# A two-layer hybrid decoder step on one Trainium2 core: the product of Y and its gate Z in the SSD stage moves from GpSimd to VectorE

## The chip, the core and the metric

The kernel runs on one core of one Trainium2 chip. The metric is the device time of one execution in microseconds (us); lower is better. "TensorE clock" below is the granted clock of a stretch as a share of full speed: it has two levels, 1.2 and 2.4 GHz, so 1.00 means 2.4 GHz throughout and 0.50 means 1.2 GHz throughout.

## What is computed

One inference step of a trunk of two layers: a chunked gMLP mixer, an MLP, a Mamba-2 (SSD) mixer, an MLP, each with RMSNorm and adaLN shift, scale and gate. 256 prompt rows and 64 sample rows (8 sequences of 8) go through the same weights, so the kernel holds 320 columns (T = 320) at a time. The change is in the Mamba-2 mixer:

```
zxbcdt = h @ w_in
z, xbc, dt_raw = split(zxbcdt)
xs, bm, cm = split(silu(conv(xbc)))
y, new_ssm = ssd_scan(xs, dt, a, bm, cm, ssm_state)
y = y + xs * d_skip
y = y * silu(z)
yg = rms_norm(y per group of 256 channels, norm_g)
out = yg @ w_out
```

The line `y = y * silu(z)` is the one whose engine changes.

## The kernel before

All activations stand transposed, channels on the 128 partitions and the 320 rows on the free axis. Weights stream from HBM in tiles of 128 x 1024 fp32 (`raw`, a ring of 6). Each is split into a high part `whi` (ScalarE, L134) and a low part `wlo` (VectorE, L135) and multiplied in three passes, `mm3` (L299, L300, L301), into one of three PSUM banks `mm`. So every weight tile costs one ScalarE and one VectorE instruction before TensorE may use it, and a `raw` buffer comes free, and the next load may start on the queue of SyncE, when its `wlo` is made.

The SSD stage (from L561) has 8 groups of 4 heads. `convs(g)` (L763) makes the six projected tiles of a group: B, C and two X tiles through the causal convolution `conv` (L594; VectorE L608, GpSimd copies L598 to L603), and two gate tiles Z by Silu (L774). `ssd(g)` (L636) is a generator in six pieces, and the next group's `convs` steps it between its tiles, so that the scan of group g is written between the projections of group g+1. Its pieces: the C-B product (L640) and the decay matrix `bc` (loaded by L632, ScalarE L646 and L647, VectorE L648); transposes (L656, L658, L670 to L676) and their scalings (L683 to L688); chunk states (L694 to L699) and `cp` (L704); then the output Y:

- L716: TensorE adds up Y of each half in PSUM, with the recurrent `state` of the samples (`st`) as one factor.
- L727: VectorE adds `xs * d_skip`, 128 x 320, twice, into the tile Y (128 x 640).
- **L728: GpSimd multiplies Y by Z in place, 128 x 640, once per group.**
- L733: ScalarE squares Y (into Z), L735: VectorE adds the halves, and the RMS norm follows: TensorE sums (L202), VectorE makes the reciprocal root (L222 and L187 to L191, ten instructions on 128 x 3), TensorE spreads it (L197), VectorE writes the normed halves into `yst` (L739).
- L744 and L760: VectorE decays and updates the state `st` with the products of L753, and GpSimd's queue sends it out (L761).

From L850 on the finished groups are split into `hhi`/`hlo` and `yhi`/`ylo` (`ysplit`, ScalarE L830, VectorE L831) and multiplied by the output weights; the last two groups' scans run beside that. This switch is called the hand-over below.

The order of the instructions on each engine is set when the program is built: a scheduler with a time model of its own places them, engine by engine, within what the dependences allow. Moving one instruction to another engine can therefore change the order of many others. At run time each engine works through its list in order.

Of the kernel before, what the change touches and what calls it, by code (L numbers as in the profile page):

```python
# [12 lines left out]
ADD, SUB, MUL, MIN, MAX = ALU.add, ALU.subtract, ALU.mult, ALU.min, ALU.max  # L13
# [37 lines left out]
def tile_trunk(ctx: ExitStack, tc: tile.TileContext, io):  # L51
    nc = tc.nc
    pe, act, dve, pool = nc.tensor, nc.scalar, nc.vector, nc.gpsimd
# [570 lines left out]
    def yt(shape, tag, dtype=F32):  # L624
        return yp.tile(shape, dtype, tag=tag, name=nm(tag), bufs=2)
# [10 lines left out]
    def ssd(g_, st, bc, ea, B, C, X, Z):  # L636
# [71 lines left out]
        Y = yt([P, 2, T], "Y")  # L708
        for r in range(2):
# [15 lines left out]
                    mmy(slice(TP + LS * b, TP + LS * b + LS), lambda w: st[:, b, w], lambda h: cp[:, h, P + LS * b : P + LS * b + LS], False)  # L725
            dd = vec[:, V_D + 2 * g_ + r : V_D + 2 * g_ + r + 1]
            dve.scalar_tensor_tensor(Y[:, r], X[r], dd, py[:, :T], MUL, ADD)  # L727
        pool.tensor_tensor(Y, Y, Z, MUL)  # L728

        yield  # L730

# [86 lines left out]
    for hf in range(2):  # L818
        pe.transpose(pt[:, hf * P : (hf + 1) * P], stkd[:, hf, :], ident)
    act.copy(natS, pt.rearrange("p (h c) -> p h c", c=P)[:, 0:2, 64:96])  # L820
    prev = ssd(0, *group_loads(0), *cz)
    for g_ in range(1, NG):
        ld = group_loads(g_)
        cz = convs(g_, prev)
        for _ in prev:
            pass
        prev = ssd(g_, *ld, *cz)
# [238 lines left out]
```

## Time and profile before

| | |
|---|---|
| median of 3 runs | 1106.19 us (1102.05 to 1108.08) |
| the profiled execution, its own time | 1104.12 us |
| its span, first to last instruction | 1102.3 us |
| TensorE busy / weight loads | 1055.1 us (96%) / 971.5 us (88%) |
| VectorE, ScalarE, GpSimd busy | 658.6, 547.1, 315.9 us |
| mean granted TensorE clock | 0.982 |
| L728 on GpSimd | 8 instructions, 3.53 to 6.42 us each |

Times in the profile count from the span's start. A timeline row reads: start, duration, engine, line, operation, output<-inputs, shape of output<-shape of input, count; a bracket at its end gives how long the engine sat idle before it and what ended that. Durations of neighbours on one engine overlap a little, since a row also holds the write-back of its result. A row of waits reads: engine and line that waited, line it waited for, total us, times, longest.

### The profile page before, as it was taken

To read this page: it belongs to the slowest core of one execution; us is meant where nothing else is said; L and a number is where in the kernel's file an instruction comes from. 1 tells how busy PE (TensorE), PEld (TensorE's weight loads), DVE (VectorE), ACT (ScalarE), POOL (GpSimd) and SP (SyncE) were. 2 spreads that over 40 slices of the span, in tenths; PEclk is the share of its full clock that TensorE was granted. 3 is DMA by queue.
4 is the path that set the end of the run, shared out by engine and by line. 5 is a ranking of instruction groups with operands and counts; after the bars stand their busy time and mean duration, and the time that the engine had idled before them with its cause. 6 is when DMAs were issued, how large, how long until landed. Compare 5 with 4: busy or idle time off the path is not lost.

```text
span 1102.3 us, 19778 instructions
## 1 busy us (share of the span) xinstructions
PE 1055.1 (96%) x7809; PEld 971.5 (88%) x7809; DVE 658.6 (60%) x1080; ACT 547.1 (50%) x1013; POOL 315.9 (29%) x403
## 2 busy tenths in 40 slices
PE   5999999999999999999997989999899999999996
PEld 3677899889899889999996879999899899999996
DVE  3544956445744433445995898988866764443342
ACT  4443333434544433334879666787435455543331
POOL 1200124332333312113361343434325243320111
PEclk9999999999999999999998998999999999999998
DMA  8877885675777767545444555655445565444531
GB/s 330 305 234 231 282 316 186 213 245 177 239 216 219 220 219 222 169 145 194 131 149 152 204 199 191 207 200 203 144 140 183 180 216 167 153 147 143 152 95 48
DMA packets 60877, 213.97 MB, mean 194 GB/s; under 512 B 6560, under 2 KB 12128, under 8 KB 58480
## 3 DMA queue, kind: packets, MB, share of 16 engines
q1 hardware_dynamic: 58544, 200.47, 55.5%
q0 software_dynamic: 1952, 11.98, 3.1%
q8 instruction: 61, 1.00, 0.4%
q14 instruction: 32, 0.26, 0.1%
q10 hardware_dynamic: 288, 0.26, 0.1%
HBM read 199.31 MB, written 12.85 MB: 192 GB/s over the span
## 4 chain that ended last, share of the span: by engine, by line
PE 71%; ACT 8%; DVE 6%; issue 5%; DMA 4%; POOL 3%; POOLq 0%; ACTq 0%; SPq 0%; DVEq 0%
PE mm L299 19%; PE mm L301 18%; PE mm L300 18%; PE adap L157 4%; ACT bc L646 2%; ACT whi L134 2%; DVE wlo L135 2%; DVE co L608 1%; DMA bc<-rowd 1%; PE ax L716 1%; PE mm L403 1%; PE mm L404 1%; PE mm L405 1%; POOL Y L728 1%; PE ax L299 1%
## 5 line engine op out<-in xcount | busy, mean ns | idle before, releaser
L135 DVE TENSOR_TENSOR wlo<-raw,whi 128x1024 fp32r<-128x1024 f32 (+1 forms) x243 | 297.2, 1224 | 225.1 <-ACT whi L134 224.1
L134 ACT ACTIVATE whi<-raw 128x1024 fp32r<-128x1024 f32 (+1 forms) x243 | 254.8, 1050 | 277.2 <-PE mm L300 197.9
L299 PE MATMUL mm<-hhi,whi 128*128 128x320 f32 x952 | 305.4, 321 | 11.1 <-ACT cb L601 5.3
L300 PE MATMUL mm<-hlo,whi 128*128 128x320 f32 x952 | 298.8, 314 | 0.9 <-DVE hlo L831 0.8
L301 PE MATMUL mm<-hhi,wlo 128*128 128x320 f32 x952 | 298.4, 314 | 0.0
L299 PEld LDWEIGHTS mm<-hhi,whi 128*128 128x128 f32 x952 | 182.0, 191 | 29.0 <-issue 13.0
L300 PEld LDWEIGHTS mm<-hlo,whi 128*128 128x128 f32 x952 | 182.5, 192 | 2.0 <-DVE hlo L831 1.1
L301 PEld LDWEIGHTS mm<-hhi,wlo 128*128 128x128 f32 x952 | 182.0, 191 | 0.7 <-issue 0.2
L299 PE MATMUL mm<-mhi,whi 128*128 128x320 f32 x512 | 159.1, 311 | 0.0
L301 PE MATMUL mm<-mhi,wlo 128*128 128x320 f32 x512 | 158.1, 309 | 0.0
L300 PE MATMUL mm<-mlo,whi 128*128 128x320 f32 x512 | 157.9, 308 | 0.0
L350 POOL TENSOR_TENSOR ta<-ta 128x320 f32<-128x320 f32 x64 | 81.5, 1275 | 142.3 <-ACT ta L348 126.8
L299 PEld LDWEIGHTS mm<-mhi,whi 128*128 128x128 f32 x512 | 96.1, 188 | 4.1 <-issue 4.1
L300 PEld LDWEIGHTS mm<-mlo,whi 128*128 128x128 f32 x512 | 96.1, 188 | 0.0
L301 PEld LDWEIGHTS mm<-mhi,wlo 128*128 128x128 f32 x512 | 96.1, 188 | 0.0
L285 POOL TENSOR_TENSOR x<-x,rs 128x64 f32<-128x64 f32 x28 | 12.1, 431 | 222.8 <-DVE rs L284 222.8
L351 ACT ACTIVATE mhi<-ta 128x320 fp32r<-128x320 f32 x64 | 30.1, 470 | 79.1 <-POOL ta L350 79.1
L352 DVE TENSOR_TENSOR mlo<-ta,mhi 128x320 fp32r<-128x320 f32 x64 | 34.7, 548 | 53.7 <-ACT mhi L351 53.7
L608 DVE SCALAR_TENSOR_TENSOR co<-cb,vec,co 128x344 f32<-128x344 f32 x96 | 54.5, 580 | 7.4 <-ACT co L606 7.2
L157 PE MATMUL adap<-raw,sc 128*32 128x256 f32 x640 | 52.9, 390 | 0.2 <-DMA raw<-ada_w 0.2
L602 POOL COPY cvp<-cb 128x3 f32<-128x3 f32 x32 | 24.1, 753 | 70.3 <-ACT cb L600 70.2
L282 DVE SCALAR_TENSOR_TENSOR x<-mm,mod,x 128x256 f32<-128x256 f32 x29 | 14.0, 483 | 46.5 <-PE mm L301 45.2
(340 smaller groups left out, 1752.0 us busy)
## 6 DMA issues: line engine op xcount, KB each, us to landing
raw<-mlp_w SPq DMA_DIRECT2D x128, 512.0 KB, 3.9
raw<-ada_w SPq DMA_DIRECT2D x80, 512.0 KB, 4.4
raw<-w_in SPq DMA_DIRECT2D x48, 512.0 KB, 3.6
raw<-ada SPq DMA_DIRECT2D x16, 512.0 KB, 5.9
raw<-gm_wv SPq DMA_DIRECT2D x16, 512.0 KB, 5.5
raw<-gm_wu SPq DMA_DIRECT2D x16, 512.0 KB, 5.5
raw<-gm_wo SPq DMA_DIRECT2D x16, 512.0 KB, 4.5
st<-state SPq DMA_DIRECT2D x8, 1024.0 KB, 5.5
```

The costliest lines, as they stand in the source:

```text
L134: act.activation(hi[:, :n], raw[:, :n], AF.Copy)
L135: eng.tensor_tensor(lo[:, :n], raw[:, :n], hi[:, :n].bitcast(F32), SUB)
L157: pe.matmul(ps[32 * j : 32 * j + 32, :256], lhsT=sc[:, k, :], rhs=r[:, j * 256 : (j + 1) * 256], start=(k == 0), stop=(k == KD - 1), skip_ ...
L299: pe.matmul(ps[:, :n], lhsT=whi[:, kk, :], rhs=hi, start=first, stop=False)
L300: pe.matmul(ps[:, :n], lhsT=whi[:, kk, :], rhs=lo, start=False, stop=False)
L301: pe.matmul(ps[:, :n], lhsT=wlo[:, kk, :], rhs=hi, start=False, stop=last)
L350: pool.tensor_tensor(s, t, t, MUL)
L351: act.activation(mhi[:, m, :], s, AF.Copy)
L352: dve.tensor_tensor(mlo[:, m, :], s, mhi[:, m, :].bitcast(F32), SUB)
L602: pool.tensor_copy(cvp[:, ct, :], cb[:, TP : TP + 3])
L608: dve.scalar_tensor_tensor(o[:, :CO], cb[:, k : k + CO], wv(k), o[:, :CO], MUL, ADD)
L646: act.activation(bc[:, h, cq[c]], bc[:, h, cq[c]], AF.Relu, bias=nat[:, c, HG * g_ + h : HG * g_ + h + 1], scale=-1.0)
```

## The change

One line: the product is issued on VectorE's queue instead of GpSimd's. Shapes, operands and result are the same.

```diff
             dve.scalar_tensor_tensor(Y[:, r], X[r], dd, py[:, :T], MUL, ADD)
-        pool.tensor_tensor(Y, Y, Z, MUL)
+        dve.tensor_tensor(Y, Y, Z, MUL)
```

The scheduler orders other instructions anew from the first group's Y on. Three places matter below; + is a row of the changed program, - one of the program before, the others stand in both.

VectorE at the end of group 0 and the start of group 1. `cp` is the scaled C, `st` the state, `ta` the sum of squares (L735), `cbm` the masked C-B product.

```order
 L704 TENSOR_TENSOR cp_6174<-ea_5497,Ct_5609 128x768
 L608 SCALAR_TENSOR_TENSOR co_6448<-cb_6441,vec,co_6448 128x344
+L728 TENSOR_TENSOR Y_5787<-Y_5787,Z_5378 128x640
 L760 TENSOR_TENSOR st_5488<-st_5488,ax_5899 128x2x256
 L760 TENSOR_TENSOR st_5488<-st_5488,ax_5901 128x2x256
 L760 TENSOR_TENSOR st_5488<-st_5488,adap_5902 128x2x256
 L760 TENSOR_TENSOR st_5488<-st_5488,ax_5900 128x2x256
-L735 TENSOR_TENSOR ta_5874<-Z_5378 128x320
 L608 SCALAR_TENSOR_TENSOR co_6448<-cb_6441,vec,co_6448 128x344
 L642 TENSOR_TENSOR cbm_5972<-ax_5968,cst 128x320
```

The product stands behind `cp` and ahead of the state's updates, and the sum of squares moves back, to three rows beyond this piece.

ScalarE at the hand-over. `hhi` and `yhi` are high parts of the finished groups, `Z<-Y` is the square (L733) of group 6, `Z_8286` a gate tile of group 7.

```order
-L830 ACTIVATE hhi<-yst_5248 128x320 x5
-L733 ACTIVATE Z_7864<-Y_8319 128x640
-L830 ACTIVATE hhi<-yst_5248 128x320 x2
+L830 ACTIVATE hhi<-yst_5248 128x320 x7
 L134 ACTIVATE whi_8589<-raw_8587 128x1024
 L774 ACTIVATE Z_8286<-mm_8373 128x320
 L830 ACTIVATE hhi<-yst_5248 128x320
+L733 ACTIVATE Z_7864<-Y_8319 128x640
 L830 ACTIVATE yhi<-yst_5249 128x320 x4
```

The square moves back by five instructions: it now stands behind all eight `hhi`, a weight split and the gate tile.

ScalarE in group 2, where the gate of group 3 (`Z_6598`) is made from the banks `mm_6599` and `mm_6685`; `cb_6797` is a convolution input, `Bn`, `Bst` and `dup` are copies for group 2's scan.

```order
-L774 ACTIVATE Z_6598<-mm_6599 128x320
-L774 ACTIVATE Z_6598<-mm_6685 128x320
+L134 ACTIVATE whi_6966<-raw_6964 128x1024
+L600 COPY cb_6797<-mm_6766 128x256
+L601 COPY cb_6797<-mm_6766 128x8x8
 L660 COPY Bn_6467<-adap_6462 128x256
 L662 ACTIVATE Bst_6469<-adap_6462,cst 128x256
 L574 COPY dup_6878<-Bt_6387 128x256
 L574 COPY dup_6880<-Xt_6515 128x256
+L774 ACT_TABLE_LOAD
+L774 ACTIVATE Z_6598<-mm_6599 128x320
```

The gate tile, which frees a PSUM bank for TensorE, moves back behind seven instructions.

## Rows read from the trace of the kernel before

**Rows 1.** The page: busy time, share of the span and instructions of each engine.

```profile
PE 1055.1 (96%) x7809; PEld 971.5 (88%) x7809; DVE 658.6 (60%) x1080; ACT 547.1 (50%) x1013; POOL 315.9 (29%) x403
```

**Rows 2.** Busy us by stretch: PE, PEld, DVE, ACT, POOL, clock, DMA share, GB/s.

```profile
607.00:776.00 169.00, 160.23 (x1482) 150.53 (x1481) 149.89 (x269) 121.35 (x271) 65.90 (x94) 0.96 0.58 201
776.00:814.00 38.00, 34.29 (x293) 31.70 (x292) 27.77 (x54) 13.38 (x28) 8.99 (x5) 0.96 0.38 128
814.00:1078.00 264.00, 263.85 (x1826) 259.05 (x1825) 140.98 (x199) 122.58 (x194) 76.00 (x81) 1.00 0.50 158
656.00:668.00 12.00, 11.62 (x46) 10.22 (x46) 10.01 (x14) 8.72 (x21) 4.69 (x5) 0.57 0.46 173
784.00:792.00 8.00, 5.12 (x28) 5.03 (x27) 5.38 (x10) 4.63 (x10) 0.74 (x2) 0.79 0.26 98
```

**Rows 3.** What TensorE waited for from 607 to 814 us.

```profile
PE mm L299 <- ACT Z L774: 4.7, 2, 2.9
PE ax L640 <- DVE st L760: 2.0, 2, 1.6
PE nrm L197 <- DVE nv L191: 1.4, 2, 1.1
PE adap L672 <- DVE Bst L663: 1.4, 1, 1.4
PE nrm L202 <- DVE ta L735: 1.3, 2, 0.9
PE mm L300 <- DVE hlo L831: 0.8, 1, 0.8
```

**Rows 4.** Timeline of GpSimd: the product in groups 0, 4 and 6.

```profile
608.00 3.54 POOL L728 TENSOR_TENSOR Y<-Y,Z 128x640 f32<-128x640 f32 x1 [2.91 <-DVE Y L727]
...
714.45 4.42 POOL L728 TENSOR_TENSOR Y<-Y,Z 128x640 f32<-128x640 f32 x1 [1.85 <-DVE Y L727]
...
777.74 6.42 POOL L728 TENSOR_TENSOR Y<-Y,Z 128x640 f32<-128x640 f32 x1 [3.85 <-DVE Y L727]
```

**Rows 5.** Timeline of VectorE beside it: state decay and cp, groups 0 and 4.

```profile
607.83 2.29 DVE L744 TENSOR_TENSOR st<-st,ea 128x2048 f32<-128x2048 f32 x1
610.03 2.32 DVE L704 TENSOR_TENSOR cp<-ea,Ct 128x768 f32<-128x768 f32 x1
...
714.29 2.28 DVE L744 TENSOR_TENSOR st<-st,ea 128x2048 f32<-128x2048 f32 x1
...
716.49 0.95 DVE L704 TENSOR_TENSOR cp<-ea,Ct 128x768 f32<-128x768 f32 x1
```

**Rows 6.** VectorE: another product of two SBUF tiles, smaller.

```profile
615.15 0.48 DVE L735 TENSOR_TENSOR ta<-Z 128x320 f32<-128x320 f32 x1
```

**Rows 7.** Timeline of ScalarE in group 5 and at the hand-over.

```profile
751.08 0.74 ACT L733 ACTIVATE Z<-Y 128x640 f32<-128x640 f32 x1 [4.41 <-POOL Y L728]
...
776.55 2.06 ACT L830 ACTIVATE hhi<-yst 128x320 fp32r<-128x320 f32 x5
784.19 0.74 ACT L733 ACTIVATE Z<-Y 128x640 f32<-128x640 f32 x1 [5.58 <-POOL Y L728]
784.84 0.81 ACT L830 ACTIVATE hhi<-yst 128x320 fp32r<-128x320 f32 x2
785.55 1.04 ACT L134 ACTIVATE whi<-raw 128x1024 fp32r<-128x1024 f32 x1
786.50 0.41 ACT L774 ACTIVATE Z<-mm 128x320 f32<-128x320 f32 x1
```

**Rows 8.** Timeline of VectorE and of TensorE at the hand-over.

```profile
780.64 2.09 DVE L831 TENSOR_TENSOR hlo<-yst,hhi 128x320 fp32r<-128x320 f32 x5
...
781.18 0.41 PE L300 MATMUL mm<-hlo,whi 128*128 128x320 f32 x1 [0.83 <-DVE hlo L831]
...
786.97 0.64 PE L299 MATMUL mm<-hhi,whi 128*128 128x320 f32 x1 [2.88 <-ACT Z L774]
```

**Rows 9.** What the DMA queue of SyncE waited for from 607 to 814 us.

```profile
SPq L145 <- DVE wlo L135: 85.5, 16, 12.6
...
SPq L629 <- DMA o_ss<-st: 16.1, 6, 4.0
```

## The prediction, made before the changed kernel ran

> **What bounds the kernel now.** I read the busy times first: TensorE is busy 96% of the span, so only what makes TensorE wait, or run at its lower clock, can be won or lost [rows 1]. Then the stretches. From the first Y at 607 us to the hand-over at 776 us TensorE is busy 160.2 of 169 us, and VectorE is close behind with 149.9; from 776 to 814 us TensorE is busy 34.3 of 38; from 814 to 1078 us 263.85 of 264 [rows 2]. So the change can act between 607 and 814 us alone: there lie 12.5 us without TensorE work (8.8 + 3.7). The clock adds something: 0.96 in both stretches, and its worst piece, 656 to 668 us, has 0.57, which costs 12 x 0.43 = 5.2 us against full clock; the piece from 784 to 792 us has 0.79, that is 8 x 0.21 = 1.7 us [rows 2]. Then what TensorE waits for: most of it is VectorE's work, and the longest single wait, 2.9 us, is for a gate tile from ScalarE [rows 3]. Last I followed the product itself with its two neighbours.
>
> **Why the product is long on GpSimd.** It takes 3.54 us in group 0, 4.42 in group 4 and 6.42 in group 6 for the same 640 elements [rows 4]. In group 0 it starts at 608.00 while VectorE runs the state's decay, which ends at 610.12; the product ends at 611.54, 1.42 us after that. VectorE's next instruction, `cp`, starts at 610.03 and takes 2.32 us, while the same instruction takes 0.95 us in group 4 [rows 5]. So one waits for the other: the product for the decay, then `cp` for the product. In group 4 `cp` goes first and the product pays. In group 6 it starves behind a chain of VectorE products until 782.73 and ends at 784.16 [rows 4, 8]. The Trainium skill ("SBUF — State Buffer", section "Who interferes with whom") says that a VectorE instruction with two SBUF inputs and a GpSimd instruction that reads SBUF exclude each other for the whole instruction. These rows agree, to within the 0.95 against 2.32 us.
>
> **The change, step by step.**
>
> *Removed: 8 GpSimd products.* GpSimd is not what anything else waits for, except through the two effects below. Its queue keeps the copies of `conv` and the DMA of the state (L761), which now starts no later than VectorE's last update plus one or two copies: cost nothing, since the load of the next state that waits for it (6 waits, 16.1 us [rows 9]) also moves behind one more weight load in the new order, and its use moves later with the scan. If that cover fails, one wait of up to 4.0 us per group is exposed.
>
> *Added: 8 VectorE products of 128 x 640.* The trace has no such row. From below: 128 x 320 takes 0.48 us [rows 6]; from above: 128 x 768 takes 0.95 us [rows 5]. Between them, by elements, 0.48 + 320 x 0.47/448 = 0.82 us. I take 0.82, nearer the larger. Eight make 6.6 us.
>
> *Returned: the block on `cp`.* 2.32 - 0.95 = 1.37 us in each of groups 0 to 3 (four such rows of 2.31 or 2.32; group 0's and a free one are shown [rows 5]), 5.5 us in all. In groups 0 to 3 VectorE thus gains 1.37 - 0.82 = 0.55 us each. The updates of the state come that much earlier, and TensorE's two waits for them (1.6 and 0.4 us [rows 3]) shrink by 0.55 and 0.4: **-1.0 us**.
>
> *Groups 4 and 5.* Nothing is returned there; VectorE's list grows by 0.82 us each. What waits behind it on that engine are `wlo` tiles, and the loads behind those (85.5 us of waiting in 16 [rows 9]). At least 0, at most 1.6 us; since VectorE has about a tenth of the time idle and the new order moves `wlo` tiles forward, I take the middle, **+0.8 us**.
>
> *The hand-over, group 6.* Before, the square of group 6 stands in ScalarE's list ahead of two `hhi`, a weight split and a gate tile, and ScalarE sits 5.58 us until GpSimd is done. The gate tile ends at 786.9 and TensorE, which needs its bank, stands 2.88 us [rows 7, 8]; then it runs at 0.79 for a while (1.7 us). In the new order the square stands behind these. Seven `hhi` at 0.41, a split of 1.04 and a gate of 0.41 from 776.55 end at about 780.9, before TensorE needs the bank. What is late next is `hlo`: VectorE's product stands ahead of the seven, so TensorE's wait of 0.83 us grows by 0.82. Sum: -2.88 - 1.7 + 0.82 = **-3.8 us**. The two waits, 0.83 and 2.88, are all of the 3.7 us that TensorE is idle from 776 to 814 us, and later it has none to speak of [rows 2], so this stays won.
>
> *The norm chain.* The square no longer waits for GpSimd (4.41 us of ScalarE in group 5 [rows 7]), and the new order puts the sums (L202) and the spread (L197) later among the weight products. Their waits on VectorE are 1.3 and 1.4 us [rows 3]. I count the first as gone and half of the second, **-2.0 us** (bounds 0 and -2.7), since in group 1 the spread now stands inside the small products of L716 and may wait there.
>
> *Gate tiles of groups 2 to 4.* They move back on ScalarE behind work worth some 3 us. The wait for them is 4.7 - 2.88 = 1.8 us, once, now [rows 3]. I leave it as it is; bounds 0 and 2 x 1.8.
>
> *The clock.* The fall at 656 us follows the small products of L716 and a wait of 1.1 us for the norm chain. In the new order that place has no such wait, but group 1 has a like one. One fall stays: 0, with bounds -5.2 and +5.2.
>
> **Sum:** -1.0 + 0.8 - 3.8 - 2.0 = -6.0 us. Against the profiled execution's own 1104.1 that is 1098.1. The median of the runs shown stands 2.1 us above that execution, so I give 1100.2 for the median.
>
> **Rivals.**
>
> *Given back inside the stage (no change that can be told).* The hand-over is won, but the scheduler's new order, which rests on a time model and not on this chip, costs elsewhere: the gate tiles wait twice as long (+1.8), the norm chain keeps its waits (+2.0 against my sum), one more fall of the clock (+5.2 at most). For it: in the stretch to 776 us three engines are close to each other [rows 2], so an order that helps one hurts another. Against it: the waits that TensorE has now are mostly on VectorE, which does not get more work there. Time: with +3.8 it is 1104.0; with the half of a clock fall, 1106.6.
>
> *VectorE sets the pace (slower).* Place: groups 0 to 5, the queue of `wlo` tiles. VectorE is busy 149.9 of 169 us. If `cp` is not released, because GpSimd's copies for the convolutions take the place of the product, all of 6 x 0.82 = 4.9 us comes on top; every microsecond delays a `wlo` and the load behind it, and TensorE's stops bring one or two more falls of the clock (+5.2 each). With the hand-over won, 4.9 + 10.4 - 3.8 = +11.5: 1117.7. It decides from the point where TensorE's waits on `wlo` (none in [rows 3]) appear. The Trainium skill ("Perfetto Trace Analysis", section "Optimizing Scalar/DVE Operations") speaks against the change in the same sense: where VectorE is saturated, some work may better go to another engine, GpSimd included; the same paragraph doubts the pair VectorE and GpSimd because they share a port. By the first half the eight products alone would cost 6.6 us; by the second, nothing. The rows on `cp` side with the second half in four groups of eight.
>
> *The clock is won too (faster).* The fall at 656 us goes and no other comes: -6.0 - 5.2 = -11.2, 1095.0.
>
> That the product stays on GpSimd is ruled out by the order of the changed program.
>
> **How the numbers follow.** A measurement of this kernel can tell about 0.5% from no change, 5.5 us. Faster by more means below 1100.7. The sum as it stands and the case with the clock: 0.34 and 0.14, together 0.48. Given back: 0.38. VectorE sets the pace: 0.14. The range runs from 1093 (the clock case with the remaining waits for VectorE gone, -2) to 1108.5 (given back, with most of a clock fall); it leaves out most of the slower case and little at the bottom. My forecast lies close to the border, which is why the two first chances are near each other.
>
> **What would show it.** After: eight VectorE rows of 128 x 640 at about 0.82 us; all `cp` near 0.95; no ScalarE wait on GpSimd's Y; at the hand-over one TensorE wait of about 1.6 us for `hlo` in place of 0.8 and 2.9; VectorE's busy time up by about 1 us over the stage; TensorE idle between the first Y and 814 us down from 12.5 to about 8. It is wrong if TensorE's waits for gate tiles grow past 4.7 us in total, if it waits for `wlo` in the SSD stage, or if more stretches at half clock appear than the two above.

## The result and the profile after

| | kernel before | changed kernel |
|---|---|---|
| median, us | 1104.31 (19 runs, 1098.20 to 1111.41) | 1111.52 (19 runs, 1106.44 to 1118.31) |
| profiled execution: own time / span / granted clock | 1104.12 / 1102.3 / 0.982 | 1114.71 / 1112.9 / 0.974 |

The ratio of after to before is 1.0067, 95% interval 1.0046 to 1.0088: the change costs about 7.3 us, where I had forecast a gain of 6.0; the median lies above my range too. The profiled execution lies 3.2 us above its kernel's median, so its trace overstates the loss a little. Over 19 runs the kernel before has 1104.31 us, 1.9 us less than the median of three from which I had forecast. Two executions, one of e5 below (1729.5 us) and one of the kernel before (1690.6 us), ran at a clock of 0.62 and 0.56 and are left out of every ratio and mean.

The page of the changed kernel, busy time by engine [rows 1]:

```profile
PE 1064.4 (96%) x7809; PEld 980.3 (88%) x7809; DVE 662.0 (59%) x1088; ACT 547.8 (49%) x1013; POOL 281.6 (25%) x395
```

The stretches [rows 2], then two halves of the stage and three places in it (columns as there: PE, PEld, DVE, ACT, POOL, clock, DMA share, GB/s):

```profile
607.00:776.00 169.00, 156.27 (x1318) 146.37 (x1317) 139.13 (x252) 113.83 (x253) 38.42 (x80) 0.90 0.56 190
776.00:814.00 38.00, 37.54 (x343) 35.77 (x343) 34.72 (x68) 19.61 (x42) 5.57 (x11) 1.00 0.44 154
814.00:1078.00 264.00, 263.88 (x1860) 257.78 (x1859) 141.80 (x202) 120.25 (x192) 71.77 (x78) 0.99 0.50 159
...
600.00:720.00 120.00, 112.10 (x969) 103.91 (x968) 97.92 (x173) 80.97 (x180) 27.09 (x58) 0.89 0.55 189
720.00:840.00 120.00, 114.59 (x1023) 108.59 (x1020) 96.33 (x181) 67.01 (x137) 19.37 (x41) 0.94 0.50 173
...
688.00:704.00 16.00, 16.00 (x134) 14.73 (x135) 12.11 (x22) 9.66 (x23) 2.54 (x7) 0.68 0.41 132
760.00:772.00 12.00, 7.42 (x38) 7.45 (x39) 7.87 (x16) 9.08 (x18) 3.21 (x6) 0.72 0.58 188
816.00:832.00 16.00, 16.00 (x139) 14.03 (x138) 12.36 (x17) 4.95 (x7) 0.55 (x2) 0.79 0.22 69
```

The same two halves in the kernel before:

```profile
600.00:720.00 120.00, 113.19 (x1077) 104.69 (x1077) 107.55 (x186) 82.17 (x183) 46.15 (x64) 0.94 0.58 199
720.00:840.00 120.00, 113.93 (x987) 108.93 (x986) 92.94 (x175) 71.48 (x145) 36.90 (x48) 0.99 0.51 175
```

From 600 to 840 us TensorE is idle 12.9 us before (240 less 113.19 and 113.93) and 13.3 after: nearly the same, with 1992 matmuls after where there were 2064. The clock is what differs. 120 x 0.06 + 120 x 0.01 = 8.4 us before and 120 x 0.11 + 120 x 0.06 = 20.4 us after are the time that it takes away in these two rows. From 688 to 704 us TensorE has work all the time and runs at 0.68, so for most of it at the lower of its two levels (1.2 of 2.4 GHz).

What TensorE waited for from 607 to 814 us, after [rows 3]:

```profile
PE nrm L202 <- DVE ta L735: 5.7, 2, 4.7
PE ax L640 <- DVE st L760: 2.7, 2, 2.5
PE mm L299 <- ACT cb L601: 2.0, 1, 2.0
PE mm L299 <- ACT Z L774: 1.8, 2, 1.3
PE ax L694 <- ACT Bn L660: 1.0, 1, 1.0
```

Of the hand-over's waits 0.5 us is left, but the hand-over comes later: ScalarE's first `hhi` starts at 788.51 us, before at 776.55 [rows 7], so the time is lost ahead of it. One wait for the norm chain has come, 4.7 us in group 5. Its story, in the timelines of VectorE, ScalarE and TensorE after [rows 7]:

```profile
753.41 0.54 DVE L727 SCALAR_TENSOR_TENSOR Y<-Xt,vec,ax 128x320 f32<-128x320 f32 x1
753.87 2.28 DVE L744 TENSOR_TENSOR st<-st,ea 128x2048 f32<-128x2048 f32 x1
756.07 0.95 DVE L704 TENSOR_TENSOR cp<-ea,Ct 128x768 f32<-128x768 f32 x1
756.94 0.82 DVE L728 TENSOR_TENSOR Y<-Y,Z 128x640 f32<-128x640 f32 x1
...
757.83 3.40 ACT L646 ACTIVATE bc<-bc,nat 128x128 f32<-128x128 f32 x12 [4.69 <-DMA bc<-rowd]
761.14 1.04 ACT L134 ACTIVATE whi<-raw 128x1024 fp32r<-128x1024 f32 x1
762.08 0.41 ACT L774 ACTIVATE Z<-mm 128x320 f32<-128x320 f32 x1
762.40 0.72 ACT L733 ACTIVATE Z<-Y 128x640 f32<-128x640 f32 x1
...
788.51 3.11 ACT L830 ACTIVATE hhi<-yst 128x320 fp32r<-128x320 f32 x7 [1.01 <-PE mm L301]
...
764.58 1.41 PE L202 MATMUL nrm<-ones_g,ta 128*128 128x1 f32 x6 [4.73 <-DVE ta L735]
```

The product itself is as short as forecast (0.82 us; `cp` has 0.95), but the order put L744 and L704 ahead of it, and on ScalarE all twelve L646, which wait 4.69 us for a transfer, ahead of the square. Y is done at 753.95 (753.41 + 0.54) and the square starts at 762.40, 8.45 us later; 3.81 of them pass until the product is done (757.76), the rest in ScalarE's list. Before, with the long product on GpSimd between them, Y was done at 746.55 and the square started at 751.08 [rows 7], 4.5 us later:

```profile
745.55 1.00 DVE L727 SCALAR_TENSOR_TENSOR Y<-Xt,vec,ax 128x320 f32<-128x320 f32 x2
```

### The profile page after: what moved, and what is told of

Read it like the earlier page. It is cut to its first block, busy times and chain, and to the rows that moved or that the text cites. A ratio compares the mean times of both kernels' runs of the same rounds, so it can differ in the third digit from the quotient of the medians.

```text
span 1112.9 us, 19804 instructions
## 1 busy us (share of the span) xinstructions
PE 1064.4 (96%) x7809; PEld 980.3 (88%) x7809; DVE 662.0 (59%) x1088; ACT 547.8 (49%) x1013; POOL 281.6 (25%) x395
## 4 chain that ended last, share of the span: by engine, by line
PE 80%; ACT 6%; DMA 4%; DVE 3%; issue 3%; POOL 2%; POOLq 0%; SPq 0%; ACTq 0%
PE mm L299 21%; PE mm L301 20%; PE mm L300 20%; PE adap L157 4%; PE ax L716 2%; ACT bc L646 1%; DMA bc<-rowd 1%; ACT whi L134 1%; PE mm L403 1%; DVE wlo L135 1%; PE mm L404 1%; PE mm L405 1%; PE ax L299 1%; PE ax L301 1%; PE ax L300 1%
## 5 line engine op out<-in xcount | busy, mean ns | idle before, releaser
L299 PEld LDWEIGHTS mm<-hhi,whi 128*128 128x128 f32 x952 | 183.3, 193 | 28.6 <-issue 13.8
L602 POOL COPY cvp<-cb 128x3 f32<-128x3 f32 x32 | 19.4, 606 | 108.9 <-ACT cb L600 108.7
```

Source lines behind the costliest of these rows:

```text
L299: pe.matmul(ps[:, :n], lhsT=whi[:, kk, :], rhs=hi, start=first, stop=False)
L602: pool.tensor_copy(cvp[:, ct, :], cb[:, TP : TP + 3])
```

## The experiments

Ratios are to runs of the kernel before on the same chip, with the 95% interval; "clock" is the granted clock averaged over the span and over a kernel's runs. Before: 0.983.

| run | product on | order | median us | ratio | clock |
|---|---|---|---|---|---|
| before | GpSimd | old | 1104.31 | 1 | 0.983 |
| changed | VectorE | new | 1111.52 | 1.0067 [1.0046, 1.0088] | 0.976 |
| e1 | VectorE | old | 1099.09 | 0.995 [0.993, 0.9971] | 0.983 |
| e2 | GpSimd | new | 1111.09 | 1.0058 [1.0034, 1.0082] | 0.978 |
| e3 | VectorE | new, gate chain early | 1109.91 | 1.0053 [1.0032, 1.0074] | 0.978 |
| e4 | VectorE | new, L202 later | 1110.85 | 1.0073 [1.0046, 1.01] | 0.980 |
| e5 | VectorE | new to group 4, then old | 1105.53 | 1.0015 [0.9996, 1.0034] | 0.980 |
| e6 | VectorE | old to group 4, then new | 1103.81 | 1.0009 [0.9992, 1.0027] | 0.982 |
| e7 | VectorE | new, L716 spread | 1109.71 | 1.0054 [1.0034, 1.0075] | 0.981 |
| e8 | VectorE | old, L716 spread | 1100.27 | 0.9959 [0.9942, 0.9977] | 0.984 |
| e9 | VectorE | new in groups 2 to 4 alone | 1102.02 | 0.9982 [0.9961, 1.0003] | 0.983 |
| e10 | VectorE | e3 and e7 together | 1108.57 | 1.0026 [1.0004, 1.0048] | 0.983 |
| e11 | VectorE | third (hint in the source) | 1095.42 | 0.9921 [0.989, 0.9953] | 0.987 |
| e12 | VectorE | new, one wait filled | 1111.10 | 1.0049 [1.0023, 1.0075] | 0.978 |
| e13 | GpSimd | third | 1099.36 | 0.9958 [0.9936, 0.998] | 0.984 |
| e14 | VectorE | fourth (two halves) | 1098.98 | 0.9953 [0.9932, 0.9974] | 0.986 |

### Engine and order apart (e1, e2)

An order can be written down: a list of instructions for each engine, and between neighbours in it a dependency that fixes their order without a wait. "Old" is the order of the kernel before, "new" that of the changed one. In the traces of e1 and e2 every engine's list is that order but for the eight products.

```diff
         tile_trunk(tc, io)
+        pinned(tc, nc, json.loads(zlib.decompress(base64.b85decode(ORDER))))
...
+def pinned(tc, nc, order):
+    place = {i.name: i for i in nc.cur_bb.bb.instructions}
+    for names in order:
+        for a, b in zip(names, names[1:]):
+            tc.add_manual_dep(place["I-%d" % b], "I-%d" % a, mybir.DependencyInfo(mybir.DependencyClass.NoSync, mybir.DependencyReason.DATA), reason="pinned")
```

> The product runs on VectorE, and every engine's instructions stand in the order of the kernel before; the eight products stand right behind the second L727 of their group. Theory A (the new order that the scheduler made costs the time, the engine does not): as before or up to 6 us faster, ratio 0.994 to 1.000, the granted clock of 607 to 776 at 0.95 to 0.97 as before, cp at 0.95 us and no wait of ScalarE for GpSimd. Theory B (VectorE has 6.6 us more to do and sets the pace): slower by 5 to 8 us in the old order too, ratio 1.005 to 1.007, with waits of TensorE for wlo or for xd, xe, cp. Theory C (the clock fell by itself, whatever the order): the clock of 607 to 776 anywhere from 0.90 to 0.97.

> The product runs on GpSimd as before, and every engine's instructions stand in the order of the changed kernel; the eight products stand in GpSimd's queue behind the instruction that they followed before. Theory A: slower than before by 7 to 12 us, ratio 1.006 to 1.011 (the new order's 7 and no gain at cp and at the hand-over), with the granted clock of 607 to 776 near 0.90 and TensorE's waits for ta L735 and cb L601 as in the changed kernel. Theory B: as before within 3 us, since VectorE has the 6.6 us back, ratio 0.997 to 1.003. Theory C: the clock of 607 to 776 anywhere from 0.90 to 0.97.

Both runs speak for theory A, e2 by a hair below its range (1.0058, where it said 1.006 to 1.011). In the old order the engine alone brings 0.5%, 5.5 us; in the new order the kernel is as slow with the product on GpSimd as with it on VectorE, so VectorE's extra work (theory B) is not the cause. That an order written down costs nothing by being written down is seen in the new order alone, where e2, e4 and e12 lie within 0.2% of the changed kernel; no run has the old order written down with the product on GpSimd. The trace of e1, first the two halves:

```profile
600.00:720.00 120.00, 112.42 (x1072) 105.61 (x1072) 103.81 (x188) 80.80 (x182) 25.80 (x58) 0.93 0.55 197
720.00:840.00 120.00, 117.44 (x1015) 113.11 (x1014) 99.97 (x186) 74.84 (x152) 26.67 (x51) 0.99 0.52 180
```

All that TensorE waited for from 776 to 840 us in e1:

```profile
PE mm L300 <- DVE hlo L831: 1.7, 1, 1.7
```

Group 5 of e1 in the timelines of VectorE and ScalarE:

```profile
745.18 1.00 DVE L727 SCALAR_TENSOR_TENSOR Y<-Xt,vec,ax 128x320 f32<-128x320 f32 x2
746.22 0.82 DVE L728 TENSOR_TENSOR Y<-Y,Z 128x640 f32<-128x640 f32 x1
...
747.08 0.74 ACT L733 ACTIVATE Z<-Y 128x640 f32<-128x640 f32 x1 [0.77 <-DVE Y L728]
```

Here the clock is that of before (0.93 and 0.99 against 0.94 and 0.99), the second half has 2.6 us without TensorE work against 6.1, and at the hand-over one wait of 1.7 us for `hlo` stands where 0.83 and 2.88 us stood [rows 8]. The square starts 0.90 us after Y. The trace of e2 has the new order's clock, with GpSimd in it:

```profile
600.00:720.00 120.00, 111.74 (x915) 103.35 (x913) 97.71 (x164) 77.78 (x171) 39.52 (x59) 0.86 0.54 182
720.00:840.00 120.00, 115.62 (x1048) 109.51 (x1045) 99.46 (x182) 69.51 (x145) 39.15 (x47) 0.97 0.51 176
```

### Where in the order it lies (e5, e6, e9)

The lists are given in words here.

```diff
-ORDER = new
+ORDER = new up to the product of group 4, then the rest in the old order
...
-ORDER = new
+ORDER = old up to the product of group 4, then the rest in the new order
...
-ORDER = new
+ORDER = old up to the product of group 2, new up to that of group 4, then old
```

> Product on VectorE; the new order up to the product of group 4, the old order from there on. By the traces of the changed kernel and of the old order with the product on VectorE, the changed kernel is 3.5 to 6.5 us behind at group 4's product and another 8 to 9 at the end. If each part of the order has its own price: 1102.5 to 1106 us, ratio to before 1.000 to 1.003, with the falls of the clock at 664 to 704. If the loss is one place (group 5's norm sum): 1098 to 1101, ratio 0.995 to 0.998.

> Product on VectorE; the old order up to the product of group 4, the new order from there on. If each part of the order has its own price: 1104 to 1108 us, ratio to before 1.001 to 1.005, with the wait for ta L735 near 760 and the fall of the clock behind it. If the early groups hold the loss: 1098 to 1102, ratio 0.995 to 0.999.

> Product on VectorE; old order up to the product of group 2, new order from there to the product of group 4, old order behind it. The new order up to group 4 cost 7.2 us (0.995 to 1.0015). If the price lies at group 3's row of small products and the fall of the clock behind it: 4 to 6 us of it, ratio to before 0.998 to 1.001. If it lies in groups 0 and 1 (waits for cb L601 and ta L735 near 608 to 648): ratio 0.995 to 0.997.

The parts add up. Against e1 the first part of the new order costs 1.0015 - 0.995, 7.2 us, the last part 1.0009 - 0.995, 6.5 us, together 13.7; the whole new order costs 1.0067 - 0.995, 12.9 us. Groups 2 to 4 hold 0.9982 - 0.995, 3.5 us, of the first part's 7.2. By the intervals each of these differences can be some 3 us off, so the 7.2 and the 6.5 are clear of zero and the 3.5 barely is. Both parts cost time, so it is not one place.

### The suspects one by one (e3, e4, e7, e8, e12), and two together (e10)

e3, the chain early, shown for group 3 (VectorE, then ScalarE; groups 0 to 5 alike, each square at its old place):

```diff
 L727 x2
-L744
-L704
 L728
+L744
+L704
 L739 x2
 L760 x3
+L735
 L760
 L135
-L735
...
+L733
 L646 x2
 L134
 L600
 L601
-L733
 L647
```

> The changed kernel with the new order on TensorE, GpSimd and SyncE, but in groups 0 to 5 the gate chain stands early: the product L728 right behind the group's second L727 (in the new order L744 and L704, 3.2 us of VectorE, mostly stand between them), the square L733 among the twelve L646 at its old place instead of behind all of them, the sum L735 ahead of the last L760. Theory A1 (the new order costs its time because the square and the sum come late for TensorE's L202): the 4.7 us wait at 764 and the fall of the clock behind it go, 1102 to 1107 us, ratio to before 0.998 to 1.003. Theory A2 (the cost lies in TensorE's own order, which of its small products L716, transposes and sums stand side by side): 1108 to 1112 us, ratio 1.004 to 1.007, the falls of the clock at 648 to 672 and 688 to 704 as in the changed kernel.

e4, TensorE alone:

```diff
-L202 x3
 L299, L300, L301 x5
+L202 x3
```

> The changed kernel in its new order, but the three L202 of groups 0 to 5 stand 15 projection matmuls (some 5 us) later on TensorE; nothing else moves. Theory A1: TensorE's 5.7 us of waits for ta L735 go, with the clock that falls behind the one at 764: 5 to 8 us faster than the changed kernel, 1103 to 1107 us, ratio to before 0.999 to 1.004. Theory A2: at most the 1 us wait at 645 and part of the one at 764 come back, 1108 to 1111 us, ratio 1.004 to 1.007. If the norm chain's later end holds up something else (yst L739, the splits L830 behind it), no gain or a loss.

Neither can be told from the changed kernel. In the profiled execution of e3 the idle time from 600 to 840 us does fall, to 9.3 us, but the clock stays: 16.0 us busy of 16 at 0.68 from 688 to 704 us, as in the changed kernel.

```profile
688.00:704.00 16.00, 16.00 (x144) 14.04 (x141) 14.57 (x29) 9.57 (x25) 2.93 (x7) 0.68 0.45 165
```

e7 in the new order (groups 2 and 3), e8 in the old one (groups 0 and 2, where 48 are cut in 24 and 24), TensorE alone:

```diff
-L716 x36
+L716 x18
+L299, L300, L301 x3
+L716 x18
+L299, L300, L301 x3
 L753 x4
```

> The changed kernel in its new order; on TensorE alone, in groups 2 and 3, the run of 36 small products L716 is cut in two with nine projection matmuls (about 3 us) between the halves and nine ahead of the L753 that follow. In the traces the granted clock falls right behind that run in group 3 in five of six kernels with the new order there, and in none of three with the old one. Theory C2 (the clock falls where the small products L716, L753 and L197 stand in one row): the falls at 664 to 672 and 688 to 704 go, 4 to 6 us less than the changed kernel, 1104 to 1107 us, ratio to before 1.000 to 1.003. Theory A1' (TensorE waits, not the clock): same as the changed kernel or slower, since L727 and the norm chain come 3 to 6 us later, ratio 1.006 to 1.010.

> Product on VectorE, every engine in the order of the kernel before, but on TensorE in groups 0 and 2, behind which the clock falls in that order, the 48 small products L716 are cut in two halves with nine projection matmuls between them and nine ahead of the L753. Theory C2: the falls at 608 to 620 and 656 to 664 go, 2 to 5 us less than the old order with the product on VectorE, 1094 to 1098 us, ratio to before 0.990 to 0.994. If it is not the row of small products: 0.995 as without the cut, or up to 1.000 where the later L727 holds up the chain.

The falls that were aimed at went in the profiled execution of e7, the time did not:

```profile
656.00:672.00 16.00, 16.00 (x175) 14.38 (x174) 13.98 (x29) 6.66 (x19) 4.46 (x11) 1.00 0.38 126
688.00:704.00 16.00, 16.00 (x172) 15.18 (x172) 13.47 (x24) 9.84 (x24) 3.32 (x8) 1.00 0.46 150
```

In its place TensorE is idle 16.0 us from 600 to 840 (240 less 109.01 and 115.02) instead of 13.3. Nor do the traces show that the edit held the clock: from 688 to 704 us it is 0.68 to 0.79 in five traces that have the new order there without the spread (changed, e2, e3, e5, e9), but 1.00 in two others without it (e4, e12), as in the two with it (e7, e10). The count in its expectation, five of six, is four of five in the traces up to e6. e8 gains nothing over e1.

e10 is e3 and e7 in one kernel.

> The changed kernel with both edits at once: the gate chain early in groups 0 to 5 on VectorE and ScalarE, and on TensorE the 36 small products L716 of groups 2 and 3 cut in two with projection matmuls between. Either alone gave 1.5 us of the 7. Theory D (waits and clock cover one another: where the clock is held, TensorE runs into the late chain, and where the chain is early, the clock still falls): together they give 5 to 8 us, 1103 to 1106 us, ratio to before 0.999 to 1.002. Theory E (the price of the new order lies elsewhere, spread over many small places): 2 to 3 us together, 1108 to 1109 us, ratio 1.004 to 1.005.

1.0026 lies between D and E and below either edit alone, with intervals that touch. Its mean clock is that of before. Of the 12.9 us between the new order and the old, these two edits return 4.5.

e12 keeps the new order and puts matmuls that nobody reads into the wait of group 5:

```diff
-    def mean_rstd(q, ones, last=False):
-        ps = nrm_ps()
+    def mean_rstd(q, ones, last=False, fill=0):
+        ps = nrm_ps(); WARM.extend(pe.matmul(ps[:, P : P + T], lhsT=hhi[:, 0, :P], rhs=hhi[:, 1, :], start=True, stop=True, skip_group_check=True).ins for _ in range(fill))
...
-        pr = mean_rstd(q1, ones_g, g_ == NG - 1)
+        pr = mean_rstd(q1, ones_g, g_ == NG - 1, 12 if g_ == 5 else 0)
```

> The changed kernel in its order, with 12 matmuls of 320 columns that nobody reads put ahead of group 5's L202 on TensorE, where it waits 4.7 us for ta L735 and the granted clock then stands at 0.5 for some 4 us. Theory C (a fall that follows an idle stretch is paid in full): the clock of 760 to 772 stays near 1.00 and 2 to 3 us come back, ratio to before 1.004 to 1.005. If the fall is hidden behind other waits: the clock stays up, the time is that of the changed kernel, ratio 1.006 to 1.008. If the idle time does not bring the fall: the clock falls all the same.

```profile
688.00:704.00 16.00, 16.00 (x132) 15.19 (x128) 11.33 (x16) 10.62 (x26) 2.57 (x6) 1.00 0.48 150
760.00:772.00 12.00, 12.00 (x85) 11.88 (x84) 11.33 (x27) 10.11 (x22) 4.13 (x8) 1.00 0.71 273
```

At 760 the clock stays at 1.00 where it was 0.72, as the first two cases said, and TensorE waits 0.24 us for `ta` instead of 4.73. The ratio does not tell these two cases apart. That the filling held the clock is likely but not shown: e2, e3, e4, e6 and e7, which have the new order there, have 0.72 to 0.88 from 760 to 772 us, but e10 has 1.00 without filling, and the execution profiled is the fastest of e12's twelve (1103.54 us, median 1111.10). The first of the two rows is the more telling one: nothing ahead of group 5's L202 differs from the changed kernel, and yet the clock is 1.00 there instead of 0.68. A fall at a given place of a given order comes in some executions and not in others. The two profiled executions of this order, the changed kernel's and e12's, differ by 11.1 us of span (1112.9 and 1101.8), and from 600 to 840 us the clock takes 20.4 us in the one and 8.4 in the other (120 x 0.07, halves at 0.93 and 1.00).

That makes the runs themselves a measurement, since each lists its span and its mean clock. The changed kernel's 19 runs have spans of 1104.7 to 1116.5 us and clocks of 0.982 to 0.971, the longer the lower (correlation -0.84). Over 292 runs of all kernels, each taken around its own kernel's mean, 0.001 of clock goes with 0.69 us. After against before, the mean clock is 0.9757 against 0.9830: 7.3 x 0.69 = 5.0 of the 8.3 us between the mean spans (1110.6 and 1102.3). Against e1 (0.9834, 1096.8) it is 7.7 x 0.69 = 5.3 of 13.8.

### Other orders (e11, e13, e14)

e11 is one line of source, a hint that queues the decay L744 behind the product; the scheduler is free in the rest. e14 is the product in halves, each behind its L727.

```diff
-        dve.tensor_tensor(Y, Y, Z, MUL)
+        yz = dve.tensor_tensor(Y, Y, Z, MUL)
...
-        dve.tensor_tensor(st.rearrange("p b (h e) -> p b h e", e=HD), st.rearrange("p b (h e) -> p b h e", e=HD), dec, MUL)
+        with tc.issue_after(yz.ins):
+            dve.tensor_tensor(st.rearrange("p b (h e) -> p b h e", e=HD), st.rearrange("p b (h e) -> p b h e", e=HD), dec, MUL)
```

```diff
             dve.scalar_tensor_tensor(Y[:, r], X[r], dd, py[:, :T], MUL, ADD)
-        dve.tensor_tensor(Y, Y, Z, MUL)
+            dve.tensor_tensor(Y[:, r], Y[:, r], Z[:, r], MUL)
```

> An edit of the source alone, with no order written down: the product on VectorE, and L744, which the new order put between the second L727 and the product, is queued behind the product. The scheduler is free in all else and makes a third order. Theory A (the order it happens to make decides): any time between the two orders seen, 1099 to 1112 us, ratio 0.995 to 1.007, and by the granted clock and TensorE's waits in 600 to 840 of its own trace it can be told which. If the product's place right behind L727 is what counts: 1099 to 1102, ratio 0.995 to 0.998.

> The product on GpSimd, every other instruction in the third order (the one that the hint behind the product brought); the eight products stand in GpSimd's queue behind the instruction that they followed before. If the engine is worth what it was worth in the old order: 5 to 6 us slower than the same order with VectorE, 1100 to 1102 us, ratio to before 0.997 to 0.998, with waits behind GpSimd for the square L733 and cp at 2.3 us again. If, as in the new order, nothing waits for the product: 0.991 to 0.994.

> An edit of the source alone: the product on VectorE in two instructions of 320 columns, each traced right behind its L727; the scheduler is free and makes a fourth order. VectorE has some 0.1 to 0.2 us a group more to do, 1 us in all. Theory A (the order it happens to make decides): anywhere from 0.990 to 1.010. If the product's early place is what counts, as in the third order: 0.991 to 0.996.

e11 has the lowest median of the study, 0.8% below before; its interval still overlaps those of e1 and e14. Its two halves:

```profile
600.00:720.00 120.00, 112.70 (x1079) 105.73 (x1075) 104.04 (x189) 82.80 (x186) 26.73 (x62) 0.96 0.58 199
720.00:840.00 120.00, 119.51 (x1017) 113.23 (x1017) 103.72 (x191) 73.91 (x154) 30.32 (x56) 1.00 0.54 182
```

The clock takes 4.8 us (120 x 0.04), the idle time is 7.8. e13 puts the product back on GpSimd in that order: 0.9958, some 4 us slower, between the two cases expected. e14, yet another order, gives 0.9953. So with the product on VectorE four orders give 0.992, 0.995, 0.995 and 1.007. A late chain alone is not what sets the new order apart: in e14 too L744 and L704 stand ahead of the second half and all twelve L646 ahead of the square, in groups 0 to 5.

## Why the prediction was wrong

- **The product, 0.82 us.** Right: 815 to 821 ns in all eight; VectorE's busy time rose 3.4 us over the span, where about 1 us was forecast for the stage.
- **`cp` released.** Right: 0.95 us in all eight.
- **Groups 4 and 5, `wlo`.** TensorE waits for no `wlo`; the queue's waits on it are 93.7 us in 19 against 85.5 in 16 [rows 9]. The rival "VectorE sets the pace" got the sign, for the wrong reason: e1 has the same VectorE work and is faster than before.
- **The hand-over, -3.8.** Right in kind: TensorE is busy 37.54 of 38 us at clock 1.00. "So this stays won" does not hold in this trace: from 816 to 832 us the clock has 0.79, which takes 3.4 us, where before it was 1.00. The wait of about 1.6 us for `hlo`, which I derived, came as 1.7 us in e1; in the new order it did not come at all.
- **State updates, -1.0.** Wrong: 2.0 us of waits became 2.7.
- **Gate tiles, 0.** Right: 1.8 us in two waits. A wait of 2.0 us for a convolution input (L601) came that no term of the sum held.
- **The norm chain, -2.0: a failed step.** "The square no longer waits for GpSimd" is true, and the waits on the chain went from 2.7 us (1.3 and 1.4) to 5.7, because the product now stands behind L744 and L704, and the square in ScalarE's list behind twelve L646 that wait for a transfer. I looked at the releaser that went, not at what the new order put ahead. So TensorE's idle time from 607 to 814 us did not fall from 12.5 us to about 8: it is 13.2 (12.73 + 0.46).
- **The clock, "one fall stays: 0": in this trace the larger failed step.** In the two rows of the halves it takes 20.4 us against 8.4, and by the runs' mean clocks about 5 of the 8.3 us go with it. I bounded it by one fall, 5.2 us; the trace after has several more of them (648, 664, 688, 760 and 816 us), which is what the prediction had named as a sign of being wrong.
- **The sum.** Its -6.0 lies close to what e1 measures, -5.5, which is what the product's engine is worth in the old order. That is luck: the terms were worked out for the new order, and in e1 they do not come out one by one. From 600 to 840 us the waits on the norm chain (2.6 us against 2.7) and on the state (2.1 against 2.0) stay; of the terms' waits only the hand-over's shrink, from 3.7 to 1.7. What I had not priced is that the changed kernel is another draw of the order. The rival "given back" named it (the order rests on a time model), and stopped at half a fall of the clock.

What stays open: some 8 of the 13.8 us by which the new order's mean span lies above the old one's do not go with the clock, and the edits tried (e3, e4, e7, e12) return no part that could be told by itself; e3 and e7 together (e10) return some 4.5. By what way the order costs them is not shown. The loss as a whole is spread over the groups (e5, e6).

## What to carry to other kernels

Where a scheduler orders the instructions, a change of engine is two changes: price them apart by writing down the old order with the new engine, before judging the idea. A gain of half a per cent is smaller than what two orders of the same work differ by (1.2% between new and old here), so a small hint that draws another order, tried a few times, can be worth more than the change. For a chain that an in-order engine waits for, look at everything that the new order puts ahead of it, and at what that in turn waits for.

## What was not expected of the hardware

In the third order GpSimd's product takes three lengths, about 2.2, 3.5 and 4.4 us. Here is group 2 of e13, GpSimd and VectorE:

```profile
662.11 2.21 POOL L728 TENSOR_TENSOR Y<-Y,Z 128x640 f32<-128x640 f32 x1 [3.31 <-DVE Y L727]
...
661.95 0.95 DVE L704 TENSOR_TENSOR cp<-ea,Ct 128x768 f32<-128x768 f32 x1
662.81 1.53 DVE L191 SCALAR_TENSOR_TENSOR nv<-nv 128x3 f32<-128x3 f32 x1
```

`cp` ends at 662.90, the product at 664.32, 1.42 us later; in the kernel before it ended 1.42 us after the decay too [rows 4, 5]. So the product needs 1.42 us by itself, and the rest of its 2.2 or 3.5 us it stands still until VectorE's instruction is through. In return an instruction of 128 x 3, which elsewhere takes 0.16 us, takes 1.53. The Trainium skill ("SBUF — State Buffer", section "Who interferes with whom") says that a VectorE instruction with two SBUF inputs contends with a GpSimd instruction that reads SBUF, that the shared ports are an exclusive lock, and that the order of issue decides who blocks. These rows agree, down to an instruction of three elements a partition.

The other surprise is that the clock's falls differ between executions of one order: 0.68 in the changed kernel and 1.00 in e12 from 688 to 704 us, where both have the same instructions behind them. And the 19 runs of the changed kernel alone have spans that differ by 11.8 us, the longer the lower their clock.
